# First layer's convolution inputs and output gate as float32 products, decays and half the key rope issued earlier

## The chip, the cores and the metric

The kernel runs on one core of one Trainium2 chip. The metric is the device time of one execution in microseconds, median of three; lower is better. Names of engines: PE is TensorE (matmul), PEld its weight load, DVE VectorE, ACT ScalarE, POOL GpSimd, SP the engine that issues nearly all DMAs.

## The reference, cut to what matters

A decoder of two layers for 256 tokens of width 1024. Each layer is a token mixer and then a SwiGLU FFN of hidden width 2816, both between RMSNorms and modulated by a conditioning vector `c` through a large weight `w_mod`.

```python
# mixer, group A: sparse attention, 8 heads x 64
idx_logits = einsum('thd,sd->ths', q_idx, k_idx)      # indexer, 8 heads
idx_score  = einsum('ths,th->ts', relu(idx_logits), w_idx)
sel        = top_k(causal(idx_score), 64)             # keys kept per query
out_a      = softmax(q.k[sel] / 8) @ v[sel]           # q, k with rotary embedding
# mixer, group B: mLSTM, 4 heads x 128, chunks of 64
qm, km     = silu(causal_dwconv(h @ W_qm)), silu(causal_dwconv(h @ W_km))
out_b      = mlstm_chunkwise(qm, km, vm, igate, log_sigmoid(fgate)) * sigmoid(h @ W_om)
y          = concat(head_norm(out_a), head_norm(out_b)) @ w_out
# FFN
y          = (silu(h @ w_gate) * (h @ w_up)) @ w_down
```

`h` is the normed and modulated input, 256 x 1024, kept as 8 blocks of 128 features. `W_qm`, `W_km` and `W_om` are column blocks of one input projection; each is 1024 x 512.

## The kernel before

**Two forms of a product.** Most products are made of three float32r matmuls: both operands are split into a high part (cast to float32r) and a low part (the difference), and `mm3` (L107 to L111) adds high x high, high x low and low x high in PSUM. `split_half` (L92 to L102) makes the parts of half a weight tile, 128x1024: the high part by ACT (L90), the low part (L101) by DVE, or by POOL where the split is marked `aside`. In the first layer the early products (values, index keys, latent queries, keys) are plain float32 products on `hf`, the unsplit `h`, with unsplit weights. Four of the products of this layer still use the split form: the two convolution inputs (`qk`, through `feat`; two weight tiles `wqk` each, PSUM m0pqk) and the output gate (`gate`, through `tok_half` and `tok`; two tiles `wom`, PSUM m0pom). For these `h` itself is split at L472 to L475 in four ACT casts and four DVE subtractions.

**Buffers.** Weight tiles of 1 MB come through the pool `ring` (7 buffers), one DMA each, issued by SP in the order of the program; a load waits until the instructions that read the tile formerly in its slot are done. Parts go to the pool `split` (5 high, 5 low). So a tile of weights that are split is free once its splits are done, a raw tile once PE has used it. PSUM has two pools of four banks.

**Order.** The mixer is cut into steps with one letter each: `e` the second half of the attention keys with the index products inside, `i` scores and top-k, `r` the key rope, `w` the mLSTM decays, `l` attention logits, `t` softmax and transposes of the weights, `u` values, `a` attended output and its norm, `q` and `k` convolution inputs, `z` silu, `m` memory, `n` recall, `s` scales, `o` gate, `g` gated, `c` and `h` transposes into the concatenation, `y` output projection; `b` and `d` are portions of a stream from `w_mod` of a later modulation (tiles `wm`, sums `macc` on DVE). The string `ORDER[0]` sets their order in the program. A step without `~` is pinned behind the last matmul of the step before; one with `~` is placed by the scheduler of the framework at build time, which fixes the order of instructions on each engine. On the chip each engine runs its list in that order, and an instruction whose operands aren't ready holds all behind it on its engine.

Names: m0 is the first layer's mixer, f0 its FFN. m0pka are attention keys in PSUM, m0pi index products, m0sc scores, m0mk the mask of the top-k, m0rka0p and m0rka0b (and 1) the two halves of the key rope on PE and DVE, m0kT the rotated keys, m0pl logits, m0lm masked logits, m0pT transposed weights, m0cv convolutions, m0W memory weights, m0num recall, m0y the projection.

## Time and profile before

| | us |
|---|---|
| median of 3 executions (754.1 to 756.5) | 754.64 |
| profiled execution | 756.11 |
| its span | 754.2 |
| PE busy | 706.8 (94%) |
| DVE busy | 569.6 (76%) |
| ACT busy | 361.3 (48%) |
| POOL busy | 120.1 (16%) |

The span runs from the first to the last instruction of the execution. An engine is busy while an instruction of it executes; a wait stands with the instruction that waited and is put down to what ended it. The granted clock of TensorE is given as a share of 2.4 GHz, so 0.5 is the level of 1.2 GHz. The prefixes h and l at the end of a weight's name are its high and low part; the digits name the tile and the half.

### The profile page before, as it was taken

How to read it: one execution, taken by the hardware profiler on the slowest of the kernel's cores; microseconds unless marked ns; L12 is line 12 of the kernel's file. 1: busy time of each engine (PE TensorE's matmuls, PEld its weight loads, DVE VectorE, ACT ScalarE, POOL GpSimd, SP SyncE). 2: the span in 40 equal slices, each digit the busy share in tenths (PEclk: the TensorE clock that was granted, in tenths of full speed). 3: DMA queues.
4: the chain of work that ended last, by engine and by line, in shares of the span. 5: the costliest groups of instructions: out<-in, count | busy, mean ns of one | idle time of the engine just before them, and what ended most of it. 6: DMA issues, size and time to landing. Idle time of an engine off the chain costs nothing.

```text
span 754.2 us, 11854 instructions
## 1 busy us (share of the span) xinstructions
PE 706.8 (94%) x4677; PEld 624.9 (83%) x4677; DVE 569.6 (76%) x870; ACT 361.3 (48%) x629; POOL 120.1 (16%) x99
## 2 busy tenths in 40 slices
PE   3989979978999999999989989999999999999996
PEld 2338748968789999999978978899879999999995
DVE  4587898997888856888797999978777576555553
ACT  6132434847474444443534543586765444444442
POOL 1000632321100013120011162633120000000020
PEclk9999978999999999999998999999999999999998
DMA  9999961265868975968785863143464587575101
GB/s 305 355 336 385 326 223 59 65 218 166 306 223 308 335 259 185 335 245 317 276 282 184 269 228 118 58 167 113 141 221 169 168 291 268 186 261 168 56 1 56
DMA packets 106156, 162.79 MB, mean 216 GB/s; under 512 B 7587, under 2 KB 83951, under 8 KB 106101
## 3 DMA queue, kind: packets, MB, share of 16 engines
q1 hardware_dynamic: 106100, 162.04, 62.8%
q8 instruction: 37, 0.61, 0.3%
q14 instruction: 19, 0.15, 0.1%
HBM read 160.98 MB, written 1.05 MB: 215 GB/s over the span
## 4 chain that ended last, share of the span: by engine, by line
PE 63%; DVE 15%; issue 9%; DMA 6%; POOL 3%; ACT 3%; SPq 0%; DVEq 0%; POOLq 0%; ACTq 0%
PE f1pu L111 8%; PE f1pg L111 8%; PE f1y L111 7%; PE f0pg L111 5%; PE f0y L111 4%; PE f0pu L111 4%; DMA wm<-in_w_mod_dram 4%; PE m1pqk L111 3%; PE m1y L111 3%; DVE macc L191 3%; PE pvm L111 2%; PE pva L111 2%; PE m0pqk L111 2%; PE m1pom L111 1%; DMA f0wd<-in_w_down_dram 1%
## 5 line engine op out<-in xcount | busy, mean ns | idle before, releaser
L191 DVE SCALAR_TENSOR_TENSOR macc<-wm,ccol,macc 128x1024 f32<-128x1024 f32 x70 | 93.9, 1341 | 9.4 <-DMA wm<-in_w_mod_dram 8.8
L258 POOL TENSOR_TENSOR macc<-macc,br 1x512 f32<-1x512 f32 x6 | 8.6, 1435 | 170.9 <-DMA br<-in_b_mod_dram 148.5
L111 PE MATMUL pvm<-m0wvm,n0hf 128*128 128x512 f32 x32 | 17.1, 684 | 7.2 <-ACT n0hf L966 5.5
L208 DVE SCALAR_TENSOR_TENSOR macc<-wq,ccol,macc 128x512 f32<-128x512 f32 x28 | 21.1, 752 | 1.2 <-DMA wq<-in_w_mod_dram 0.2
L111 PEld LDWEIGHTS pvm<-m0wvm,n0hf 128*128 128x128 f32 x32 | 6.7, 219 | 15.4 <-ACT n0hf L966 7.4
L882 ACT CAST f0th<-f0t 128x512 fp32r<-128x512 f32 x10 | 6.2, 620 | 22.7 <-DVE f0t L872 22.7
L966 ACT ACTIVATE n0hf<-n0xT,mod,A 128x256 f32<-128x256 f32 x7 | 3.9, 594 | 27.2 <-DVE A L220 27.2
L111 PE MATMUL m0pka<-n0hf,m0wka 128*128 128x256 f32 x64 | 15.9, 389 | 0.0
L111 PE MATMUL pva<-m0wva,n0hf 128*128 128x512 f32 x32 | 14.4, 592 | 0.0
L111 PEld LDWEIGHTS m0pka<-n0hf,m0wka 128*128 128x128 f32 x64 | 11.5, 190 | 3.3 <-issue 1.6
L189 DVE TENSOR_SCALAR macc<-wm,ccol 128x1024 f32<-128x1024 f32 x10 | 8.9, 888 | 6.5 <-DMA wm<-in_w_mod_dram 5.2
L872 DVE TENSOR_TENSOR f1t<-f1pu,f1s 128x512 f32<-128x512 f32 x11 | 7.6, 690 | 6.7 <-PE f1pu L111 5.2
L262 POOL TENSOR_TENSOR ml<-macc,mh 128x512 fp32r<-128x512 f32 x6 | 9.6, 1592 | 19.3 <-ACT mh L260 19.3
L111 PEld LDWEIGHTS pva<-m0wva,n0hf 128*128 128x128 f32 x32 | 6.1, 190 | 7.7 <-issue 7.2
L101 POOL TENSOR_TENSOR f0wd910l<-f0wd,f0wd910h 128x1024 fp32r<-128x1024 f32 x1 | 2.6, 2647 | 59.2 <-ACT f0wd910h L90 59.2
L354 POOL TENSOR_TENSOR m0qidx<-m0rqidx0x,cosT 128x512 f32<-128x512 f32 x1 | 1.5, 1547 | 65.1 <-ACT m0rqidx0x L90 65.1
L770 DVE SCALAR_TENSOR_TENSOR m1cv<-m1pqk,vc,m1cv 128x255 f32<-128x255 f32 (+2 forms) x24 | 11.1, 476 | 0.7 <-ACT m1cv L764 0.5
L101 POOL TENSOR_TENSOR f0wd201l<-f0wd,f0wd201h 128x1024 fp32r<-128x1024 f32 x1 | 2.4, 2409 | 57.8 <-ACT f0wd201h L90 57.8
L770 DVE SCALAR_TENSOR_TENSOR m0cv<-m0pqk,vc,m0cv 128x255 f32<-128x255 f32 (+2 forms) x24 | 10.9, 470 | 0.0
L115 PE MATMUL pm<-ident,macc 128*128 128x128 f32 x72 | 10.4, 283 | 0.4 <-ACT row L90 0.4
L115 PE MATMUL n0pt<-ident,n0xr 128*128 128x128 f32 x16 | 3.9, 428 | 7.2 <-ACT n0xr L317 7.2
L218 DVE TENSOR_REDUCE mod<-pm 128x4 f32<-128x512 f32 x4 | 2.8, 692 | 10.2 <-PE pm L115 10.2
(1917 smaller groups left out, 2978.1 us busy)
## 6 DMA issues: line engine op xcount, KB each, us to landing
wm<-in_w_mod_dram SPq DMA_DIRECT2D x40, 1024.0 KB
f0wd<-in_w_down_dram SPq DMA_DIRECT2D x11, 1024.0 KB
f1wd<-in_w_down_dram SPq DMA_DIRECT2D x11, 1024.0 KB
f0wg<-in_w_gate_up_dram SPq DMA_DIRECT2D x10, 1024.0 KB
f0wu<-in_w_gate_up_dram SPq DMA_DIRECT2D x10, 1024.0 KB
f1wg<-in_w_gate_up_dram SPq DMA_DIRECT2D x10, 1024.0 KB
f1wu<-in_w_gate_up_dram SPq DMA_DIRECT2D x10, 1024.0 KB
wq<-in_w_mod_dram SPq DMA_DIRECT2D x32, 256.0 KB
```

The lines of the kernel that those rows point to most:

```text
L101: final["lo"] = (nc.gpsimd if aside != (name in OTHER) else nc.vector).tensor_tensor(lv, raw, hv.bitcast(F32), op=ALU.subtract)
L111: final["pe"] = nc.tensor.matmul(*args, **kw)
L115: final["pe"] = nc.tensor.transpose(*args)
L189: nc.vector.tensor_scalar_mul(acc, w[:, kk, :], ccol[:, k:k + 1])
L191: nc.vector.scalar_tensor_tensor(acc, w[:, kk, :], ccol[:, k:k + 1], acc, op0=ALU.mult, op1=ALU.add)
L208: last = nc.vector.scalar_tensor_tensor(acc, w[:, kk, :], ccol[:, k:k + 1], acc, op0=ALU.mult, op1=ALU.add)
L258: nc.gpsimd.tensor_tensor(acc[0:1, :], acc[0:1, :], br[0:1, :], op=ALU.add)
L262: nc.gpsimd.tensor_tensor(lo, acc, hi.bitcast(F32), op=ALU.subtract)
L770: nc.vector.scalar_tensor_tensor(o[:, d:], s[:, :S - d], V["conv_w"][:, tap * 8 + j:tap * 8 + j + 1], o[:, d:], op0=ALU.mult, op1=ALU.add)
L872: nc.vector.tensor_mul(t, pu, s)
L882: nc.scalar.copy(th[:, 0], r3(t, 2))
L966: nc.scalar.activation(hf[:, j, :], s, AF.Identity, scale=A, bias=b)
```

## The change

`hf` takes the place of the split `h` (its tag "hh"; the tile "hl" stays, without use in this layer's mixer), the pool `ring` gets an eighth buffer, and `h` is not split. The convolution inputs and the output gate of the first layer become float32 products of `hf` and raw tiles: no parts of `wqk` and `wom` are made. `ORDER[0]` starts with the decays (`w0`) and the first half of the key rope (`r0`) ahead of the index products (`e10`, `e11`); its second half (`r1`) loses its pin, and `k00` and `q00` stand ahead of `l0`.

```diff
--- before.py
+++ after.py
@@ -57,7 +57,7 @@
 def tile_hybrid_decoder(ctx: ExitStack, tc: tile.TileContext, a, out):
     nc = tc.nc
     const = ctx.enter_context(tc.tile_pool(name="const", bufs=1))
-    ring = ctx.enter_context(tc.tile_pool(name="ring", bufs=7))
+    ring = ctx.enter_context(tc.tile_pool(name="ring", bufs=8))
     split = ctx.enter_context(tc.tile_pool(name="split", bufs=5))
     keep = ctx.enter_context(tc.tile_pool(name="keep", bufs=1))
     work = ctx.enter_context(tc.tile_pool(name="work", bufs=2))
@@ -383,13 +383,16 @@
     def tok_split(raw, nm):
         return [split_half(raw[:, 4 * g:4 * g + 4, :], f"{nm}{g}", g == 1) for g in range(2)]
 
-    def tok(ps, ws, h, tiles, inside=()):
+    def tok(ps, ws, h, tiles, inside=(), hf=None):
         step, inside, wait = 0, dict(inside), None
         for i in tiles:
             for k in range(KD):
-                w = ws[k // 4]
+                w = ws[k // 4] if hf is None else None
                 hold = tc.issue_after(wait) if wait else ExitStack()
                 with hold:
+                    if hf is not None:
+                        matmul(ps[:, i * 256:(i + 1) * 256], hf[:, k, i * P:(i + 1) * P], ws[:, k, :], start=k == 0, stop=k == KD - 1)
+                        continue
                     mm = mm3(ps[:, i * 256:(i + 1) * 256],
                              (h[0][:, k, i * P:(i + 1) * P], h[1][:, k, i * P:(i + 1) * P]),
                              (w[0][:, k % 4, :], w[1][:, k % 4, :]), k == 0, k == KD - 1)
@@ -435,7 +438,7 @@
                     first and q == 0, last and q == len(ws) - 1)
 
     HEAD = ((2, 2, 1, 1), (3, 2, 1, 0, 0))
-    ORDER = ("e10~ e11~ i0~ r0~ b1~ i1~ w0~ r1 l0~ t00~ k00~ q00~ l1 t01 q01 d u00~ l2 b1 u01 t10~ t11 u10 k01~ d a0~ q10 z0~ t20~ q11 u11 t21~ u20~ k10~ u21 k11 a1 b1 c0~ d b2~ z1~ m0 n0 o00~ c1~ o01~ m1 n1~ o10~ s0~ b1 s1 o11 g1 g0~ d h1~ h0 y0~ y2~",
+    ORDER = ("w0~ r0~ e10~ e11~ i0~ b1~ r1~ i1~ k00~ q00~ l0~ t00~ l1 t01 q01 d u00~ l2 b1 u01 t10~ t11 u10 k01~ d a0~ q10 z0~ t20~ q11 u11 t21~ u20~ k10~ u21 k11 a1 b1 c0~ d b2~ z1~ m0 n0 o00~ c1~ o01~ m1 n1~ o10~ s0~ b1 s1 o11 g1 g0~ d h1~ h0 y0~ y2~",
              "v0 i0 r0 r1~ i1 w0~ v1~ l0 k00~ l1 b1 q00 t01~ t00~ q01~ u00 t10 b0 l2~ u01~ t11~ q10 b0 k01 u10~ a0~ t20 q11~ u11 c0 u20~ t21 k10 b1~ u21 b0~ k11~ z0 m0 z1 b0 o00~ a1~ o01~ n0~ m1~ c1 n1~ o10 s0~ o11~ g0~ y0 s1 g1~ h0 h1 y2~")
 
     def mixer(l, h, between, early, hook, hf=None):
@@ -469,10 +472,6 @@
         else:
             with tc.issue_after(final["A"].ins):
                 angles()
-                for q in range(4):
-                    two = slice(2 * q, 2 * q + 2)
-                    nc.scalar.copy(h[0][:, two, :], hf[:, two, :])
-                    nc.vector.tensor_tensor(h[1][:, two, :], hf[:, two, :], h[0][:, two, :].bitcast(F32), op=ALU.subtract)
         for k in range(KD):
             if l:
                 mm3(ps[:80, :S], (hi[:, k, :], lo[:, k, :]), (h[0][:, k, :], h[1][:, k, :]), k == 0, k == KD - 1)
@@ -539,8 +538,9 @@
 
         def tok_half(key, c0, name, tile_, inside=()):
             if tile_ == 0:
-                half[key] = bankB(f"{nm}p{name}"), tok_split(load_cols(win, c0, f"{nm}w{name}"), f"{nm}w{name}")
-            tok(*half[key], h, (tile_,), inside)
+                raw = load_cols(win, c0, f"{nm}w{name}")
+                half[key] = bankB(f"{nm}p{name}"), tok_split(raw, f"{nm}w{name}") if l else raw
+            tok(*half[key], h, (tile_,), inside, hf)
             return r3(half[key][0], 2)
 
         def v_att(g, tile_, inside=()):
@@ -755,7 +755,7 @@
             if m == 0:
                 half[key] = bankB(f"{nm}pqk{which}{g}"), load_cols(win, (C_QM, C_KM)[which] + g * 256, name)
             ps, raw = half[key]
-            feat(ps, raw, h, name, True, None, (m,))
+            feat(ps, raw, h, name, True, None, (m,), (), hf)
             if m == 0:
                 return
             for m in range(2):
@@ -947,13 +947,12 @@
     little(2)
     xT = first_norm("n0")
     keep.tile([P, 16], F32, tag="edge0", name="edge0")
-    h = hh, hl = new_h("n0")
+    hf = keep.tile([P, KD, S], F32, tag="hh", name="n0hf")
+    keep.tile([P, KD, S], F32R, tag="hl", name="n0hl")
     keep.tile([P, 48], F32, tag="edge1", name="edge1")
     A0 = small.tile([P, KD], F32, tag="A1", name="A0")
     macc0 = [work.tile([P, D], F32, tag="macc", name=f"macc0{t}", bufs=2) for t in range(2)]
     early = {n: [bankB(f"p{n}{i}") for i in range(NT)] for n in ("vm", "va")}
-    hf = keep.tile([P, KD, S], F32, tag="hf", name="n0hf")
-
     for q in range(4):
         B = mod_quarter(q)
         wv = {n: r3(split.tile([P, 1024], F32, tag=t, name=f"m0w{n}{q}"), 2) for n, t in (("vm", "hi"), ("va", "lo"))}
@@ -1014,7 +1013,7 @@
 
         if l + 1 < L:
             turns_of.append(load_vectors(1))
-        y = mixer(l, h, during[l][0], early, to_ffn, None if l else hf)
+        y = mixer(l, h if l else None, during[l][0], early, to_ffn, None if l else hf)
         h = next_h(y, rowsof[l, G_M], rowsof[l, SC_F], mod_of(l, SH_F), f"nf{l}")
         y = ffn(l, h, during[l][1], nxt["w"], to_mixer)
         if l + 1 < L:
```

The scheduler places the instructions anew. On PE, from the last index product (m0pi) of the first mixer on, the list before is this (m0pu and m0pM belong to the mLSTM decays):

```order
L111 MATMUL m0pi_649<-m0kidx,m0qidx 128x256 x2
L111 MATMUL m0pka_589<-n0hf,m0wka_590 128x256 x4
L111 MATMUL m0rka0p<-m0rka0x,perm 128x512
L115 MATMUL m0pu<-ident,m0ga 128x4 x4
L111 MATMUL m0pM_743<-Mp,sel 128x256 x2
L111 MATMUL m0pM_753<-Mp,sel 128x256 x2
L111 MATMUL m0pqk_803<-n0hh,m0wqk100l 128x256
L111 MATMUL m0pqk_803<-n0hh,m0wqk100h 128x256
L111 MATMUL m0pqk_803<-n0hl,m0wqk100h 128x256
L111 MATMUL m0pqk_803<-n0hh,m0wqk100l 128x256
L111 MATMUL m0pqk_803<-n0hh,m0wqk100h 128x256
L111 MATMUL m0rka1p<-m0rka1x,perm 128x512
```

and in the changed kernel, from the same product up to the first transposes of the attention weights:

```order
L111 MATMUL m0pi_675<-m0kidx,m0qidx 128x256 x2
L111 MATMUL m0pka_615<-n0hf,m0wka_616 128x256 x4
L111 MATMUL m0pqk_762<-n0hf,m0wqk_763 128x256 x2
L111 MATMUL m0rka1p<-m0rka1x,perm 128x512
L111 MATMUL m0pqk_762<-n0hf,m0wqk_763 128x256 x3
L111 MATMUL m0pqk_773<-n0hf,m0wqk_774 128x256 x8
L111 MATMUL m0pl_787<-m0kT,m0q 128x128 x4
L111 MATMUL m0pl_793<-m0kT,m0q 128x128 x4
L111 MATMUL m0pqk_762<-n0hf,m0wqk_763 128x256 x8
L115 MATMUL m0pT_809<-ident,m0lm_786 128x128 x4
```

m0rka0p, m0pu and m0pM have gone from this place, to one ahead of the first index product; between m0rka1p and the first transposes m0pT now stand 19 steps of m0pqk on the raw tiles and eight products m0pl. On DVE, at the scores of the same mixer, the list before has m0rka0b and the copy of m0uc between the rounds of the first top-k:

```order
L665 MATCH_REPLACE m0sc_594<-m0m_666,m0sc_594 128x128
L654 SCALAR_TENSOR_TENSOR m0sc_621<-m0rl_652,m0wi,m0sc_621 128x256
L664 MAX m0m_669<-m0sc_594 128x8
L356 TENSOR_TENSOR m0rka0b<-m0rka0p,sinT 128x512
L665 MATCH_REPLACE m0sc_594<-m0m_669,m0sc_594 128x128
L357 TENSOR_TENSOR m0kT<-m0kT,m0rka0b 128x512
L664 MAX m0m_672<-m0sc_594 128x8
L611 COPY m0uc<-m0pu 128x8
L665 MATCH_REPLACE m0sc_594<-m0m_672,m0sc_594 128x128
L356 TENSOR_TENSOR m0rka1b<-m0rka1p,sinT 128x512
```

and the changed kernel has them ahead of the first score:

```order
L356 TENSOR_TENSOR m0rq0b<-m0rq0p,sinT 128x512
L356 TENSOR_TENSOR m0rq1b<-m0rq1p,sinT 128x512
L611 COPY m0uc<-m0pu 128x8
L357 TENSOR_TENSOR m0q<-m0q,m0rq1b 128x512
L356 TENSOR_TENSOR m0rka0b<-m0rka0p,sinT 128x512
L357 TENSOR_TENSOR m0kT<-m0kT,m0rka0b 128x512
L652 TENSOR_SCALAR m0sc_620<-m0rl_626,m0wi 128x128
L654 SCALAR_TENSOR_TENSOR m0sc_620<-m0rl_626,m0wi,m0sc_620 128x128
L191 SCALAR_TENSOR_TENSOR macc_498<-wm_890,ccol,macc_498 128x1024
L654 SCALAR_TENSOR_TENSOR m0sc_620<-m0rl_626,m0wi,m0sc_620 128x128
```

m0rka0b, the addition to m0kT and the copy now stand ahead of all scores, and no low part of m0wqk stands there. On DVE at the end of the mixer, from the low parts of the concatenation on (m0wo are weights of the projection, f0we early weights of the FFN), the list before is:

```order
L685 SCALAR_TENSOR_TENSOR m0cat4hl<-m0cm1p,vc_102,m0cat4hh 128x128 x4
L685 SCALAR_TENSOR_TENSOR m0cat4hl<-m0cm0p,vc_102,m0cat4hh 128x128 x4
L101 TENSOR_TENSOR m0wo200l<-m0wo_1606,m0wo200h 128x1024
L101 TENSOR_TENSOR f0we01l<-f0we_1638,f0we01h 128x1024
L101 TENSOR_TENSOR m0wo201l<-m0wo_1606,m0wo201h 128x1024
L101 TENSOR_TENSOR m0wo210l<-m0wo_1608,m0wo210h 128x1024
L101 TENSOR_TENSOR m0wo211l<-m0wo_1608,m0wo211h 128x1024
L101 TENSOR_TENSOR f0we10l<-f0we_1648,f0we10h 128x1024
L101 TENSOR_TENSOR f0we11l<-f0we_1648,f0we11h 128x1024
L302 TENSOR_TENSOR nf0yg_1708<-m0y_1534,row_1021 128x512
L189 TENSOR_SCALAR macc_2186<-wm_2187,ccol 128x1024
```

and the changed kernel's:

```order
L685 SCALAR_TENSOR_TENSOR m0cat4hl<-m0cm1p,vc_102,m0cat4hh 128x128 x4
L685 SCALAR_TENSOR_TENSOR m0cat4hl<-m0cm0p,vc_102,m0cat4hh 128x128 x4
L101 TENSOR_TENSOR f0we01l<-f0we_1389,f0we01h 128x1024
L101 TENSOR_TENSOR m0wo201l<-m0wo_1357,m0wo201h 128x1024
L101 TENSOR_TENSOR m0wo210l<-m0wo_1359,m0wo210h 128x1024
L189 TENSOR_SCALAR macc_1937<-wm_1938,ccol 128x1024
L101 TENSOR_TENSOR m0wo211l<-m0wo_1359,m0wo211h 128x1024
L101 TENSOR_TENSOR f0we10l<-f0we_1399,f0we10h 128x1024
L101 TENSOR_TENSOR f0we11l<-f0we_1399,f0we11h 128x1024
L191 SCALAR_TENSOR_TENSOR macc_1937<-wm_1938,ccol,macc_1937 128x1024
L302 TENSOR_TENSOR nf0yg_1459<-m0y_1285,row_932 128x512
```

The first macc of the tile `wm` now stands ahead of m0wo211l; before it stood behind the first product nf0yg of the next norm.

## Rows read from the trace of the kernel before

**Rows 1.** Windows: us, busy time and instructions by engine, clock, DMA.
```profile
core 0: us, PE busy (x) PEld busy (x) DVE busy (x) ACT busy (x) POOL busy (x), PEclk, DMA share, GB/s
87.00:205.90 118.90, 105.96 (x656) 90.21 (x654) 103.17 (x207) 64.28 (x145) 31.25 (x24) 0.93 0.52 177
103.50:109.00 5.50, 0.29 (x3) 0.12 (x1) 5.50 (x16) 0.00 (x0) 2.06 (x3) 0.64 1.05 356
109.00:119.00 10.00, 10.00 (x38) 7.62 (x39) 8.93 (x31) 2.92 (x10) 2.91 (x6) 0.51 0.14 42
130.00:155.00 25.00, 24.61 (x212) 23.69 (x211) 23.19 (x43) 19.25 (x40) 6.79 (x3) 1.00 0.33 113
155.00:167.00 12.00, 6.81 (x51) 6.26 (x50) 10.88 (x23) 4.71 (x12) 4.01 (x2) 0.98 0.58 206
167.00:184.50 17.50, 15.43 (x113) 14.67 (x111) 13.09 (x29) 12.35 (x32) 2.01 (x2) 0.92 0.56 182
217.10:388.00 170.90, 170.90 (x1245) 161.82 (x1245) 134.43 (x132) 78.32 (x92) 17.05 (x10) 1.00 0.80 278
```

**Rows 2.** Waits of PE from 80 to 225 us, by releaser.
```profile
engine line waited for: us in total, times, longest us
PE m0rka1p L111 <- DVE m0rka0b L356: 5.2, 1, 5.2
PE m0num L111 <- DVE m0W L785: 3.3, 1, 3.3
...
PE m0cm1p L115 <- DVE m0mo L828: 2.1, 1, 2.1
PE m0pqk L111 <- DVE m0cv L770: 1.9, 1, 1.9
```

**Rows 3.** Chain of waits, 62 to 325 us: start, duration, work.
```profile
69.48 5.61 PE m0pka L111 x26
...
108.91 2.04 PE m0rka1p L111 x2
...
123.60 0.11 PE m0pT L115
...
251.96 5.66 PE f0pg L111 x48
```

**Rows 4.** Time line of DVE in the first mixer: start, duration, instruction.
```profile
85.01 0.68 DVE L357 TENSOR_TENSOR m0qidx<-m0qidx,m0rqidx1b 128x512 f32<-128x512 f32 x1
...
87.41 1.21 DVE L101 TENSOR_TENSOR m0wqk100l<-m0wqk,m0wqk100h 128x1024 fp32r<-128x1024 f32 x1
...
91.01 2.83 DVE L357 TENSOR_TENSOR m0q<-m0q,m0rq1b 128x512 f32<-128x512 f32 x1 [1.79 <-POOL m0q L354]
...
97.06 0.27 DVE L652 TENSOR_SCALAR m0sc<-m0rl,m0wi 128x128 f32<-128x128 f32 x1
...
115.59 0.22 DVE L667 TENSOR_SCALAR m0mk<-m0sc 128x128 f32<-128x128 f32 x1
...
128.77 0.29 DVE L667 TENSOR_SCALAR m0mk<-m0sc 128x256 f32<-128x256 f32 x1
...
145.32 2.34 DVE L746 TENSOR_TENSOR m0rd<-m0rd,m0ra0r 128x8 f32<-128x8 f32 x1 [1.55 <-POOL m0ra0r L280]
```

**Rows 5.** Time line of POOL, one low part of a weight.
```profile
90.93 2.36 POOL L101 TENSOR_TENSOR m0wqk001l<-m0wqk,m0wqk001h 128x1024 fp32r<-128x1024 f32 x1
```

**Rows 6.** Chain of waits, then time line of PE, at the projection.
```profile
192.93 7.35 DMA wm<-in_w_mod_dram
...
198.20 0.40 PE L111 MATMUL m0y<-m0wo211l,m0cat4hh 128*128 128x512 f32 x1
```

**Rows 7.** Time lines of DVE, then PE, at the FFN's end.
```profile
367.56 1.23 DVE L101 TENSOR_TENSOR m1wvm00l<-m1wvm,m1wvm00h 128x1024 fp32r<-128x1024 f32 x1 [4.59 <-ACT m1wvm00h L90]
...
392.47 2.60 DVE L191 SCALAR_TENSOR_TENSOR macc<-wm,ccol,macc 128x1024 f32<-128x1024 f32 x2
394.98 1.22 DVE L101 TENSOR_TENSOR f0wd911l<-f0wd,f0wd911h 128x1024 fp32r<-128x1024 f32 x1
...
396.25 0.79 PE L111 MATMUL f0y<-f0wd911l,f0th 128*128 128x512 f32 x1 [2.91 <-DVE f0wd911l L101]
...
397.27 0.63 PE L111 MATMUL f0y<-f0wd910h,f0th 128*128 128x512 f32 x1
...
402.69 0.39 PE L111 MATMUL f0y<-f0wd910h,f0th 128*128 128x512 f32 x1
```

## The prediction, written before the changed kernel ran

> **What bounds the kernel now.** I read four views in this order. First the windows of the stretch that the change touches, the mixer of the first layer [rows 1]: from 87 to 205.9 us TensorE is busy for 105.96 of 118.9 us; most of the rest lies in 103.5 to 109 (0.29 of 5.5 us) and in 155 to 167 (6.81 of 12 us); behind the first hole the granted clock is 0.51, which is the 1.2 GHz level, through all of 109 to 119. VectorE is full in the first hole (5.50 of 5.5) and 91% busy in the second. Then the waits of TensorE [rows 2]: 5.2 us for the key's rotary product m0rka0b, 3.3 us for the memory weights m0W, 1.9 us for the convolutions m0cv, all from VectorE. So the mixer has two limits that alternate: TensorE by its amount of work, VectorE by what stands ahead of the instruction that TensorE needs. Third the chain of waits for the durations [rows 3], fourth the time lines of VectorE and GpSimd around the two holes [rows 4, 5]. Behind the mixer, the FFN from 217 to 388 us keeps TensorE busy for every microsecond [rows 1], so a gain of the mixer arrives at the end unshortened; the one hole of the FFN is at its end [rows 7].
>
> **1. TensorE gets more work: +7.5 us.** 96 products of one contraction step (64 of the convolution inputs, 32 of the output gate) change from three float32r matmuls to one float32 product. The chain has both forms with 256 columns: 13 float32 steps of m0pka (26 records) in 5.61 us, 0.432 us each; 16 steps of three of f0pg in 5.66 us, 0.354 us each [rows 3]. The difference, 0.078, times 96 is 7.5 us. The Trainium skill, "FP8 and Floating Point Precision" (TensorE Precision Notes), says that a true float32 product takes four passes; three passes in 0.354 us would make four 0.472 and the sum 11.3, an estimate by that page, 3.8 us worse than mine. The row measures the very operand kinds, partitions and columns of the new products, and it gives 0.432.
>
> **2. VectorE, ScalarE and GpSimd get less.** Twelve low parts of weights go, six on VectorE at 1.21 us (7.3 us) and six on GpSimd, as do 12 casts on ScalarE and the split of h. The split of h I cost at nothing: it lies before 87 us, where TensorE is busy without a hole for the early products. A GpSimd split also held VectorE: the add to m0q took 2.83 us beside m0wqk001l where an add of the same shape takes 0.68, and m0wqk000l stood beside the next one; m0rd, a 128x8 product, took 2.34 us beside a split of wom [rows 4, 5]. At about 2.2 us each, four such places are 8.7 us. Together VectorE loses 16 us of 103 busy between 87 and 205.9. This is no gain by itself; it counts only where TensorE waits.
>
> **3. The first hole goes: -5.**  In the new order the first half of the key rope, with decays, is issued ahead of the index products. m0rka0b then stands on VectorE ahead of the scores instead of behind the third round of the top-k, where it ran at 108.10 us. What is issued between 87 and 103.5 us on TensorE is otherwise the same work, so m0rka1p comes when the last m0pka and two steps of m0pqk are done, at about 104.4 instead of 108.91 [rows 3]. That is 4.5 us, and the half clock of the 10 us behind it (TensorE is busy there for 10.00 us at 0.51, so 4.9 us of work at full clock [rows 1]) goes as well, if no new hole takes its place.
> One does. TensorE now has ready: 11 steps of m0pqk (4.75 us), the eight m0pl (about 2) and eight more steps (3.46), which brings it to about 115. Then stand the transposes of the weights, which need the exponentials, which need mask 0 and the maximum. VectorE starts the scores at about 92 instead of 97.06, because the two blocked instructions before it are gone; it cannot finish them before the last m0pi, which is now at 101.8 (three instructions were put ahead). I get mask 0 at about 109 instead of 115.59, the maximum at 116.3, the first transposes between 117 and 118.7. So TensorE waits about 3 us there, and probably runs slowly behind it: the only 3.3 us hole of this mixer (before m0num) left 0.92 in the 17.5 us behind it, the 5.2 us hole 0.51 over 10 us [rows 1, 2]. Bounds for the new hole: 0 to 5.2 us, its half clock 0 to 4.9 us; I take 3 and 2. The first transpose was at 123.60 [rows 3] and TensorE has done the same 24 steps before it, so at this point the lead is 5 us (118.7), or 3 with the slow clock behind it.
>
> **4. The second hole shrinks.** Behind the transposes 72 of the 96 longer steps are still to come. In 130 to 155 TensorE is 98% busy [rows 1], so 40 of them lie on the path: 40 x 0.078 = 3.1 us, and the lead at the last convolution product falls from 5 to about 2. But then TensorE was waiting for VectorE: 5.19 of 12 us idle in 155 to 167. VectorE's second mask was at 128.77 [rows 4] and is now at about 118.5. In 130 to 167, up to m0W, it was busy for 34.1 us [rows 1], two blocked m0rd with 4.4 of them, so 29.7 of work; in the new order it has 2.4 us of splits of wo and 2.6 of macc more in front of m0W (they stood behind it) and 1.2 less of wom: 33.5, so it is done by 152, or by 156 with the waits it had, and the last convolution product arrives at 151 to 152 with 3 us of work behind it. m0num starts at about 156 instead of 166.5. From there TensorE had 39.2 us to the end of the output projection, 2.1 of them idle and some 1.4 lost to the clock; with 2.5 us more for the gate that is 39 to 42. The projection ends at 197 to 199 instead of 205.7.
>
> **5. A wait that the order brings in.** The slot for the weight tile wm that is loaded near the end of the mixer is freed by the low part f0we01l, and its first use on VectorE now stands two instructions behind that, ahead of m0wo211l; before it stood well behind it. That load took 7.35 us from issue to landing [rows 6]. Queued behind the waiting macc is m0wo211l, for which TensorE waits: its first use was at 198.20 [rows 6]. Moved by one low part ahead, f0we01l frees the slot at 191.54 of the old time; landing after 4 to 7.35 us (the lower end: the loads ahead of it are released earlier by TensorE now, and 1 MB at the 278 GB/s of [rows 1] takes 3.8), then 0.76 for the macc and 1.23 for the low part, gives 197.5 to 200.9. TensorE waits 0 to 2.7 us; I take 1.
> Parts 3 to 5 together: the walk gives -6.7 to -8.7, less 1. I take -6, since each of its stations assumes no wait that I have not seen; bounds 0 (all holes only move) and -10 (both holes and the half clock go).
>
> **6. The eighth ring buffer: -4.** At the end of the first FFN the last low part f0wd911l starts at 394.98, behind two macc (2.60 us), and TensorE waits 2.9 us; the matmuls behind it start 0.43 us apart until 402, then 0.227 apart, about 12 x 0.2 = 2.4 us more [rows 7]. VectorE has no hole between 367.56 and that point but 0.69 us, and the row at 367.56 shows why it is late: 4.59 us for a cast of a tile that had just landed. The ring has one buffer more, so this load can be issued one slot earlier; where slots and not the transfer rate set the time (0.80 of the DMA share in this stretch, 278 GB/s against 356 in 103.5 to 109 [rows 1]) it lands earlier. In the new order one of the two macc also stands in front of f0th, in the 0.69 us hole. Bounds: 0 (the transfers are the limit) to -5.3 (wait and slow clock go); I take -4, since two microseconds more of the 4.59 already bring the hole to the size (1.9, before m0pqk) behind which the granted clock stayed up. The second layer's mixer and FFN I cost at nothing: the code is the same there.
>
> **Sum.** The profiled execution took 756.11 us with a span of 754.2, so 1.9 us lie around the span. 756.1 - 6 - 4 = 746.1 by that execution; it stands 1.5 us above the median of 754.64, so I forecast **744.6**.
>
> **Rivals.**
> A. The forecast, both gains in part: 741 to 749. Chance 0.50. The page's four passes would put 3.8 us on the sum and stay in this case.
> B. The eighth buffer gives nothing, as the transfers pace the FFN: only the mixer's -6, 754.64 - 6 = 748.6, say 748 to 752. For it speaks the DMA share of 0.80 with transfers of about 7 us; against it that slots are held back by VectorE, which is what waits. Chance 0.23.
> C. The hole at the transposes takes the place of the first one at full price (5.2 and 4.9 us), so the mixer gains 0 to 2, with half the buffer's gain: 750 to 754. For it speaks that TensorE runs out of ready work at 115 at the latest; against it that mask 0 is earlier by six. Chance 0.14.
> D. Slower: TensorE is the bound. The hole moves from m0rka1p to the transposes with its slow clock, as in C, and the 7.5 us of longer products stand on the path all through, since the remaining idle time (3.3, 1.9 and 2.1 us) is in places where the longer products do not fit; about half of it absorbs some. With the wait of part 5 (2.7) and no gain of the buffer: 7.5 + 2.7 - 3.6 = +6.6, 761; from 757 if a part is absorbed. It decides at one point: whether m0num comes later than 164 in spite of the lighter VectorE. Chance 0.08.
> E. VectorE was the bound all through and its 16 us count to the full: -10 and -5, 739.6. Against it TensorE's 98% in 130 to 155. Chance 0.05.
> What a measurement of this kernel can tell from no change is 0.3%, 2.3 us. Faster by more: A, E, nearly all of B (0.20) and a third of C: 0.80. Within: the rest of B and C, 0.12. Slower: 0.08. The range that leaves out D, half of E and a little more is 739.5 to 753.
>
> **What would show it.** Right: m0rka1p at about 104 with no wait; the first score at about 92, mask 0 at about 109; the granted clock near 1 in 105 to 115; m0num at about 156; the end of the projection at 197 to 199; f0wd911l no longer waited for, or for under 2 us. Wrong: a wait of the transposes of over 4 us with the lower level behind it (C); m0num after 164 (D); m0wo211l waited for by over 3 us; the wait for f0wd911l still at 2.9 (B); float32 steps of m0pqk at more than 0.45 us.

## The result: faster by 2.4%

The changed kernel takes 737.4 us (median, 735.65 to 738.5); the kernel before took 755.57 beside it. The ratio is 0.9758, 95% interval 0.9729 to 0.9787. The forecast was 744.6, the range 739.5 to 753. So the direction was right, and the gain is 18 us where 10 were forecast; the time lies 2.1 us below the range. The profiled execution has a span of 735.2 us, 19.0 less than before. The ratios in this document leave out executions over 1.5% above the fastest of their kernel (among them four of the twelve of f2 below and one of the twelve of f3), while the medians in us are of all executions.

Where the 19.0 us come from is read by following the same instructions in both traces: the last m0y ends 8.8 us earlier (197.03 for 205.83), all FFN matmuls behind the norm run 11.5 earlier, the last f0y ends 18.1 earlier (388.36 for 406.48), the last instruction 19.0. So up to the end of the mixer 8.8 us are gained, in the norm behind it 2.7, at the end of the first FFN 6.6, in the second layer 0.9. The 8.8 hold a loss of 1.8 from the start of the execution, told below; from the last matmul of pva (it ends at 57.74 for 55.93) to the end of m0y the gain is 10.6.

The windows of the kernel after, by the columns of [rows 1]; the first is its mixer from the place of the old 87 us to the end of m0y, the second the norm behind it:

```profile
core 0: us, PE busy (x) PEld busy (x) DVE busy (x) ACT busy (x) POOL busy (x), PEclk, DMA share, GB/s
88.80:197.03 108.23, 105.96 (x559) 86.44 (x558) 91.02 (x204) 54.52 (x134) 14.80 (x17) 1.00 0.63 211
197.03:205.10 8.07, 6.89 (x56) 6.43 (x57) 7.54 (x19) 7.41 (x19) 1.10 (x2) 1.00 0.62 216
106.70:119.00 12.30, 11.58 (x59) 9.18 (x58) 11.85 (x40) 1.02 (x5) 1.57 (x2) 1.00 0.30 92
...
372.00:388.40 16.40, 16.36 (x73) 13.17 (x71) 11.47 (x14) 7.05 (x15) 3.51 (x3) 1.00 0.96 330
```

The mixer is 108.23 us long; the same stretch before, 87 to 205.85, was 118.85. TensorE was busy for 105.96 us of either. It was idle for 12.89 us and is for 2.27: the shortening is idle time, all of it. That busy time has not grown although the products are longer goes, by an estimate from these rows, to the clock: it was 0.93 over the stretch of [rows 1] and is 1.00 now, and 7% of 106 us is 7.4, about the 7.5 us of the longer products. The norm takes 8.07 us for 11.25, and the end of the FFN (372 to 388.4) has no hole and the full clock. The waits of TensorE from 60 to 480 us (columns as in [rows 2]), against those there and in [rows 7]:

```profile
PE nf0pt L115 <- DVE nf0xr L332: 1.2, 2, 0.7
...
PE m0pT L115 <- ACT m0lm L711: 0.7, 1, 0.7
...
PE m0cm1p L115 <- DVE m0mo L828: 0.4, 1, 0.4
```

The 5.2, 3.3 and 1.9 us are gone, 2.1 has become 0.4, and the 2.9 us at the end of the FFN are gone too. TensorE's stations, for [rows 3] (start and duration of a group; the idle time before it in brackets):

```profile
106.70 1.13 PE L111 MATMUL m0rka1p<-m0rka1x,perm 128*128 128x512 f32 x2
...
118.53 1.48 PE L115 MATMUL m0pT<-ident,m0lm 128*128 128x128 f32 x4 [0.66 <-ACT m0lm L711]
...
154.08 0.83 PE L111 MATMUL m0num<-m0vm,m0W 128*128 128x129 f32 x6
```

and VectorE's, for [rows 4], at the index products and at the end of the mixer:

```profile
91.01 1.26 DVE L357 TENSOR_TENSOR m0q<-m0q,m0rq1b 128x512 f32<-128x512 f32 x1
...
94.24 0.42 DVE L652 TENSOR_SCALAR m0sc<-m0rl,m0wi 128x128 f32<-128x128 f32 x1
...
110.77 0.21 DVE L667 TENSOR_SCALAR m0mk<-m0sc 128x128 f32<-128x128 f32 x1
...
178.43 1.21 DVE L101 TENSOR_TENSOR f0we01l<-f0we,f0we01h 128x1024 fp32r<-128x1024 f32 x1
182.88 1.23 DVE L101 TENSOR_TENSOR m0wo201l<-m0wo,m0wo201h 128x1024 fp32r<-128x1024 f32 x1 [3.24 <-ACT m0wo201h L90]
...
185.38 0.75 DVE L189 TENSOR_SCALAR macc<-wm,ccol 128x1024 f32<-128x1024 f32 x1
```

The add to m0q is down from 2.83 to 1.26 us, the first score at 94.24, mask 0 at 110.77. All of these times hold 1.8 us from the start of the execution: eight early matmuls of pvm took 5.40 us where before they took 3.70. The first line is from the kernel before, the others are from the changed kernel, the last with the columns of [rows 1]:

```profile
39.52 3.70 PE L111 MATMUL pvm<-m0wvm,n0hf 128*128 128x512 f32 x8 [1.81 <-ACT n0hf L966]
...
39.63 5.40 PE L111 MATMUL pvm<-m0wvm,n0hf 128*128 128x512 f32 x8 [1.87 <-ACT n0hf L965]
...
39.60:43.00 3.40, 3.37 (x5) 1.35 (x6) 3.26 (x5) 0.47 (x1) 0.00 (x0) 0.55 1.01 340
```

So the lag is the lower level of the clock (0.55 over 3.4 us) behind a hole of 1.87 us; before, the hole was 1.81 us and the clock stayed at 1.00. Whether it comes from the change is open: of the nine traces in which no split `h` is made (the changed kernel and the runs e1, e2, e5, e6, f1, f2, f3 and g1 below), all have the hole of 1.87 us, but seven have the 5.40 us and two, f2 and g1, have 3.70; the five traces that split `h` have 1.81 and 3.70.

### The profile page after: what moved, and what is told of

The parts are those of the page before. It is cut to its first block, busy times and chain, and to the rows that moved or that the text cites. A ratio compares the mean times of both kernels' runs of the same rounds, so it can differ in the third digit from the quotient of the medians.

```text
span 735.2 us, 11619 instructions
## 1 busy us (share of the span) xinstructions
PE 702.1 (95%) x4581; PEld 618.8 (84%) x4581; DVE 550.9 (75%) x860; ACT 348.3 (47%) x613; POOL 106.3 (14%) x93
## 4 chain that ended last, share of the span: by engine, by line
PE 80%; DVE 11%; ACT 3%; issue 3%; POOL 1%; DMA 1%; SPq 0%; DVEq 0%; POOLq 0%; ACTq 0%
PE f1pu L111 8%; PE f0pu L111 8%; PE f0pg L111 8%; PE f1pg L111 8%; PE f1y L111 7%; PE f0y L111 7%; PE m1pqk L111 3%; PE m1y L111 3%; PE pvm L111 3%; PE m0y L111 2%; PE pva L111 2%; PE m0pka L111 2%; PE m1pva L111 2%; PE m1pom L111 1%; PE m1pka L111 1%
## 5 line engine op out<-in xcount | busy, mean ns | idle before, releaser
L191 DVE SCALAR_TENSOR_TENSOR macc<-wm,ccol,macc 128x1024 f32<-128x1024 f32 x70 | 96.1, 1373 | 9.5 <-DMA wm<-in_w_mod_dram 8.8
L111 PE MATMUL m0pqk<-n0hf,m0wqk 128*128 128x256 f32 x128 | 29.6, 382 | 0.0
L111 PEld LDWEIGHTS m0pqk<-n0hf,m0wqk 128*128 128x128 f32 x128 | 23.8, 190 | 3.6 <-issue 0.5
L111 PEld LDWEIGHTS pvm<-m0wvm,n0hf 128*128 128x128 f32 x32 | 7.1, 234 | 16.4 <-ACT n0hf L965 7.7
L111 PE MATMUL m0pom<-m0wom,n0hf 128*128 128x256 f32 x64 | 14.5, 379 | 0.0
L111 PEld LDWEIGHTS m0pka<-n0hf,m0wka 128*128 128x128 f32 x64 | 11.5, 190 | 3.3 <-issue 1.6
L111 PEld LDWEIGHTS m0pom<-m0wom,n0hf 128*128 128x128 f32 x64 | 11.9, 190 | 1.4
L711 ACT ACTIVATE m0lm<-m0lm,m0mx 128x128 f32<-128x128 f32 (+1 forms) x16 | 7.1, 445 | 12.2 <-DVE m0mx L708 12.2
```

The costliest lines, as they stand in the source:

```text
L111: final["pe"] = nc.tensor.matmul(*args, **kw)
L191: nc.vector.scalar_tensor_tensor(acc, w[:, kk, :], ccol[:, k:k + 1], acc, op0=ALU.mult, op1=ALU.add)
L711: final["exp"] = nc.scalar.activation(lm[:, g, :], lm[:, g, :], AF.Exp, bias=mx[:, g:g + 1], accum_out=den[:, hd:hd + 1])
```

## Experiments

Each kernel was timed in turns with the kernel before on the same chip; the ratio to it is what is compared (medians of before lie between 753.9 and 755.6 us).

| run | products | order string | buffers | else | us | ratio (95%) |
|---|---|---|---|---|---|---|
| changed kernel | float32 | new | 8 | | 737.4 | 0.9758 (0.9729 to 0.9787) |
| e1_ring7 | float32 | new | 7 | | 745.0 | 0.9869 (0.9832 to 0.9905) |
| e2_oldorder | float32 | old | 8 | | 737.6 | 0.9767 (0.9736 to 0.9798) |
| e3_before_neworder | split | new | 7 | | 757.4 | 1.0028 (1.0004 to 1.0052) |
| e5_f32only | float32 | old | 7 | | 745.4 | 0.9884 (0.9848 to 0.9920) |
| f1_keep_all | float32 | old | 7 | all splits made, and six that the kernel before lacks | 765.8 | 1.0149 (1.0116 to 1.0181) |
| f2_keep_pool | float32 | old | 7 | GpSimd's splits made, and three more | 756.8 | 0.9995 (0.9962 to 1.0028) |
| f3_keep_dve | float32 | old | 7 | VectorE's splits made, and three more | 750.4 | 0.9935 (0.9902 to 0.9969) |
| h1_conv_only | float32 in conv | old | 7 | | 750.6 | 0.9937 (0.9912 to 0.9962) |
| h2_gate_only | float32 in gate | old | 7 | | 750.6 | 0.9934 (0.9908 to 0.9960) |
| e6_ring6 | float32 | new | 6 | | 743.5 | 0.9847 (0.9806 to 0.9888) |
| g1_ring7_macc_last | float32 | new | 7 | last macc late | 738.3 | 0.9784 (0.9756 to 0.9812) |
| i1_before_macc_last | split | old | 7 | last macc late | 750.4 | 0.9953 (0.9930 to 0.9977) |

### Which part of the change: products, order or buffer

```diff
e1:  -ring bufs=8  +ring bufs=7                       (of the changed kernel)
e2:  -ORDER[0] new +ORDER[0] of before                (of the changed kernel)
e3:  -ORDER[0]     +ORDER[0] of the changed kernel    (of the kernel before)
e5:  e1 and e2 together
```

e1_ring7. 

> The changed kernel with 7 ring buffers instead of 8. Theory (the buffer makes the gain at the end of the first FFN, the rest of the change makes that of the mixer): the wait for f0wd911l returns with 2 to 3.5 us and a slow clock behind it, the end of the projection m0y stays near 197 us; 741 to 745 us, 4 to 7 above the changed kernel's 737.4. Rival (the macc moved ahead of f0th, or the earlier start of the stream, makes the gain at the FFN's end): no wait there, 737 to 739 us.

e2_oldorder. 

> The changed kernel with the order string of before (float32 products and 8 buffers stay). Theory (products and order share the mixer's gain, since the lighter VectorE reaches m0rka0b earlier even where it stands among the top-k rounds): a hole of 1 to 3 us before m0rka1p, m0num near 158 to 160, the FFN's end without a wait; 740 to 744 us. Rival (the order alone makes the mixer's gain, the longer products only cost): the hole of 5 us and the slow clock stay, 748 to 755 us.

e3_before_neworder. 

> The kernel before with the order string of the change alone (split form, 7 buffers). Theory: m0rka0b comes early and the hole of 5 us goes, but VectorE keeps its splits and its blocked instructions, so m0num waits as before; mixer 2 to 5 us shorter, the wait at the FFN's end stays: 750 to 754 us. Rival (the order alone makes the mixer's gain): the projection ends near 197 us, 743 to 748 us.

e5_f32only. 

> The float32 products alone: order string of before, 7 ring buffers. Theory: as the run with the old order and 8 buffers, but with the wait at the FFN's end: 745 to 751 us. Rival (TensorE's work bounds the mixer, 7.5 us more of it): 755 to 762 us.

The products alone give 1.2% (e5), the eighth buffer another 1.1% (e1 against the changed kernel, e5 against e2), the order nothing: with it or without it the float32 kernels are equal within their intervals, at either number of buffers, and alone (e3) it costs 0.3%. For e2 my theory still left 1 to 3 us of the hole to the order; its wait is this:

```profile
PE m0rka1p L111 <- DVE m0rka0b L356: 0.4, 1, 0.4
```

With the old order m0rka0b still stands among the top-k rounds, but VectorE gets there in time. For e3 both expectations were wrong. The first hole is gone there and three others have come, in places that had none or less before: two wait for VectorE directly, and m0pT waits for ScalarE's m0lm, which needs VectorE's mask. The third line is the FFN's end, as it was:

```profile
PE m0pqk L111 <- DVE m0cv L770: 4.9, 1, 4.9
PE m0pl L111 <- DVE m0kT L357: 3.5, 1, 3.5
PE f0y L111 <- DVE f0wd911l L101: 2.9, 1, 2.9
PE m0pT L115 <- ACT m0lm L711: 2.6, 1, 2.6
```

So the place of m0rka0b decides where TensorE waits, but gains nothing: VectorE was late, and with the new order other instructions of TensorE waited for it.

### What in the products: VectorE's own work or GpSimd's hold on it

```diff
 # e5, in feat (and alike for wom in tok_half); the parts are read by nothing
             if hf is None:
                 w = ... split_half(...)
+            elif True:          # f1; f2: m == 1 (GpSimd's), f3: m == 0 (VectorE's)
+                split_half(raw[:, :, m * P:(m + 1) * P], f"{nm}{m}", aside and m == 1)
```

f1_keep_all. 

> The float32 products alone (old order, 7 buffers; 745.4 us), and the twelve splits of wqk and wom made all the same, for nothing: six low parts on VectorE, six on GpSimd, twelve casts on ScalarE. TensorE's matmuls are those of the changed kernel. Theory (the mixer's gain is the work taken from VectorE, and TensorE's longer products only cost): the hole before m0rka1p and the wait for m0W return, 753 to 760 us. Rival (the gain comes from TensorE's side: fewer and simpler matmuls, or raw tiles freed in another order): 744 to 748 us.

f2_keep_pool. 

> As the run that keeps all splits, but only the six low parts on GpSimd with their six casts. Theory (GpSimd's splits hold VectorE for about 2.2 us each in four places): about half of the loss returns, m0q and m0rd take over 2 us again; 748 to 751 us. Rival (only VectorE's own work counts): 744 to 747 us.

f3_keep_dve. 

> As the run that keeps all splits, but only the six low parts on VectorE (1.21 us each) with their six casts. Theory: the other half, 748 to 752 us. Rival (GpSimd's blocking makes the loss): 744 to 747 us.

These three runs make more splits than their expectations count. `feat` also makes the latent queries and the attention keys, whose weights m0wcq and m0wka the kernel before never splits. So f1 makes eighteen splits and not twelve, f2 and f3 nine each and not six, and the scheduler put them at other times than in the kernel before (m0wqk011l on GpSimd at 101.73 in f2, at 119.89 before). What they show is the direction: TensorE's products are those of e5 in all three, and with split work added the gain shrinks (f3, where 0.5% are lost against e5) or is gone (f2, where 1.1% are lost, though its splits use no time of VectorE's own). What pays is the work taken away, not the form of the product. What the six splits of each engine cost they don't show: before any low part of m0wqk is made, VectorE's m0qidx already comes 3.7 us later than in e5 in f2, and 2.8 later in f3 (both counted from the last pva), where m0rka0b in the end is 6.8 and 4.2 us later. The casts on ScalarE and the buffers of `split` that these splits take were not tested apart. In f2 the wait before m0rka1p is back, larger than before; the other rows are a GpSimd split and, on VectorE, a score instruction that runs into it and the like one that doesn't:

```profile
PE m0rka1p L111 <- DVE m0rka0b L356: 6.1, 1, 6.1
...
101.73 2.36 POOL L101 TENSOR_TENSOR m0wqk011l<-m0wqk,m0wqk011h 128x1024 fp32r<-128x1024 f32 x1
...
102.00 2.37 DVE L659 SCALAR_TENSOR_TENSOR m0sc<-m0rl,m0wi,m0sc 128x256 f32<-128x256 f32 x1
...
107.09 0.47 DVE L659 SCALAR_TENSOR_TENSOR m0sc<-m0rl,m0wi,m0sc 128x256 f32<-128x256 f32 x1
```

2.37 us for 0.47: the instruction of VectorE lasts until the split of GpSimd is over. In f3 the same wait of TensorE is 2.5 us. f1 lost more than f2 and f3 together, and more than was expected, but not by the splits of the change. The pair m0wi took 0.36 us in the kernel before; in f1 it runs into GpSimd's split of m0wka and lasts 3.63, VectorE's own split of m0wka follows, m0qidx comes late by both, TensorE waits 2.75 us ahead of m0pi, and the lower clock follows; columns of the window as above:

```profile
87.82 3.63 DVE L594 TENSOR_SCALAR m0wi<-m0wif,m0rqr 128x8 f32<-128x8 f32 x2
...
87.85 2.35 POOL L101 TENSOR_TENSOR m0wka11l<-m0wka,m0wka11h 128x1024 fp32r<-128x1024 f32 x1
...
87.00:120.00 33.00, 30.25 (x80) 19.49 (x78) 30.96 (x40) 11.70 (x16) 17.68 (x11) 0.64 0.37 120
...
95.03 1.22 PE L111 MATMUL m0pi<-m0kidx,m0qidx 64*128 64x128 f32 x4 [2.75 <-DVE m0qidx L357]
96.18 2.07 PE L111 MATMUL m0pka<-n0hf,m0wka 128*128 128x256 f32 x4
```

Two float32 steps of m0pka take 2.07 us there where they take 1.06 on the chain after, and this lasts from 95 to 119 us (granted clock 0.50), so by an estimate up to 12 us of this run's loss are the clock.

### Which of the products

```diff
h1 (of before):  qk():  -feat(ps, raw, h, name, True, None, (m,))
                        +feat(ps, raw, h, name, True, None, (m,), (), hf)
h2 (of before):  tok and tok_half as in the changed kernel; qk and the split of h stay
```

h1_conv_only. 

> The kernel before with the convolution inputs alone as float32 products (h is split still, for the gate; old order, 7 buffers). Theory (the low parts of wqk stand ahead of m0rka0b, and make the first hole): nearly the whole gain of the products, hole under 1 us, 745 to 749 us. Rival (the parts of wom in the second hole count as much): 749 to 752 us.

h2_gate_only. 

> The kernel before with the output gate alone as float32 products (h and wqk split still; old order, 7 buffers). Theory: the first hole of 5 us stays, the wait for m0W falls by 2 to 3 us, TensorE has 2.5 us more: 752 to 756 us, no difference that can be told. Rival: 749 to 752 us.

Each gives about 0.65%, and together they are what e5 gives: the rivals were right. Both runs still split `h`, and e5 doesn't; nothing is left over that this split could be worth. The conv products remove the first hole (m0rka0b at 101.69 on VectorE, 2.1 us of that from an earlier start of this execution; the wait for it is 0.4 us) and leave waits further on:

```profile
PE m0pqk L111 <- ACT row L90: 2.4, 2, 2.2
...
101.69 0.67 DVE L356 TENSOR_TENSOR m0rka0b<-m0rka0p,sinT 128x512 f32<-128x512 f32 x1
```

The gate leaves the first hole as it was, and gains behind it: m0rd, which took 2.34 us beside a wom split, takes 0.17, and the waits for m0W and m0cv are gone. From the last pva its m0y ends 3.0 us earlier, and the norm behind it is 2.6 shorter, of which h1 has 0.3 (more on the norm below):

```profile
PE m0rka1p L111 <- DVE m0rka0b L356: 5.2, 1, 5.2
...
145.92 0.17 DVE L750 TENSOR_TENSOR m0rd<-m0rd,m0ra0r 128x8 f32<-128x8 f32 x1 [1.54 <-POOL m0ra0r L280]
```

### The end of the first FFN: the buffer or VectorE's list

```diff
e6:  -ring bufs=8  +ring bufs=6                       (of the changed kernel)
 # g1 (of e1) and i1 (of the kernel before), in ffn
-            between()
+            if c < NF - 2 or l:
+                between()
...
         down(NF - 2, NF - 1)
+        if not l:
+            between()
```

e6_ring6. 

> The changed kernel with 6 ring buffers (8: 737.4, 7: 745.0 us). Theory (slots, not the transfer rate, set when the FFN's tiles come): each buffer less costs about as much, the waits of TensorE in the FFN grow to 6 us or more; 752 to 765 us. Rival (7 buffers are just one short of what the end of the FFN needs and the transfer rate bounds the rest): 745 to 749 us.

g1_ring7_macc_last. 

> The changed kernel with 7 buffers (745.0 us, waits 2.9 us for f0wd911l at the end of the first FFN), and the last portion of the w_mod stream of that FFN written behind the last down product: its two macc (2.6 us) then stand behind f0wd911l on VectorE. Theory A (the wait is VectorE's queue, 27 us without a hole from the late tile m1wvm to f0wd911l; 2.6 us out of it do nearly what the eighth buffer does): wait for f0wd911l 0 to 1 us, no slow clock, 738 to 741 us. Theory B (the late tile itself, thus the slot, is what counts): the wait stays over 2 us, 743 to 746 us.

i1_before_macc_last. 

> The kernel before, with the last portion of the w_mod stream of the first FFN written behind the last down product and nothing else of the change. Theory (the wait at the FFN's end is VectorE's queue ahead of f0wd911l; the eighth buffer is one way to shorten it): no wait of TensorE there, 747 to 751 us. Rival (without the buffer or the faster mixer the tiles come too late): the wait stays over 2 us, 753 to 757 us.

With 7 buffers the wait of 2.9 us is back; first line TensorE's wait, then VectorE from the late tile on:

```profile
PE f0y L111 <- DVE f0wd911l L101: 2.9, 1, 2.9
...
358.35 1.23 DVE L101 TENSOR_TENSOR m1wvm00l<-m1wvm,m1wvm00h 128x1024 fp32r<-128x1024 f32 x1 [4.66 <-ACT m1wvm00h L90]
...
385.59 1.22 DVE L101 TENSOR_TENSOR f0wd911l<-f0wd,f0wd911h 128x1024 fp32r<-128x1024 f32 x1
```

In the changed kernel the cast of that tile is through at 347.81 and f0wd911l starts before TensorE needs it:

```profile
347.81 1.23 DVE L101 TENSOR_TENSOR m1wvm00l<-m1wvm,m1wvm00h 128x1024 fp32r<-128x1024 f32 x1 [2.39 <-ACT m1wvm00h L90]
...
377.30 1.23 DVE L101 TENSOR_TENSOR f0wd911l<-f0wd,f0wd911h 128x1024 fp32r<-128x1024 f32 x1 [0.16 <-ACT f0wd911h L90]
```

But e6, with one buffer less than e1, has no such wait, and is no slower than e1; both its expectations were wrong. From the last f0pu to the last f0y it takes 16.4 us as the changed kernel does, where e1 takes 23.4; its mixer ends 2.5 us later than that of e1 (1.0 of it from the start of the execution), its norm is 2.2 longer and its second layer 2.4. Its scheduler put a pair of macc behind f0wd911l instead of ahead of it:

```profile
365.35 1.23 DVE L101 TENSOR_TENSOR m1wvm00l<-m1wvm,m1wvm00h 128x1024 fp32r<-128x1024 f32 x1 [0.40 <-ACT m1wvm00h L90]
...
386.03 1.21 DVE L101 TENSOR_TENSOR f0wd911l<-f0wd,f0wd911h 128x1024 fp32r<-128x1024 f32 x1
...
389.32 2.61 DVE L191 SCALAR_TENSOR_TENSOR macc<-wm,ccol,macc 128x1024 f32<-128x1024 f32 x2 [0.95 <-DMA wm<-in_w_mod_dram]
```

g1 does that by hand with 7 buffers, and is as fast as the changed kernel within the intervals; TensorE waits for f0wd911l no more:

```profile
349.64 1.23 DVE L101 TENSOR_TENSOR m1wvm00l<-m1wvm,m1wvm00h 128x1024 fp32r<-128x1024 f32 x1 [0.21 <-ACT m1wvm00h L90]
...
375.78 1.22 DVE L101 TENSOR_TENSOR f0wd911l<-f0wd,f0wd911h 128x1024 fp32r<-128x1024 f32 x1 [0.16 <-ACT f0wd911h L90]
376.93 1.28 DVE L191 SCALAR_TENSOR_TENSOR macc<-wm,ccol,macc 128x1024 f32<-128x1024 f32 x1
```

i1 does it in the kernel before, with nothing else changed. The first wait, 5.2 us, and the second, 3.5, are there still as in [rows 2]; the one at the FFN's end was 2.9 us:

```profile
PE f0y L111 <- DVE f0wd911l L101: 0.2, 1, 0.2
...
363.88 1.23 DVE L101 TENSOR_TENSOR m1wvm00l<-m1wvm,m1wvm00h 128x1024 fp32r<-128x1024 f32 x1 [2.46 <-ACT m1wvm00h L90]
...
390.52 1.21 DVE L101 TENSOR_TENSOR f0wd911l<-f0wd,f0wd911h 128x1024 fp32r<-128x1024 f32 x1
```

Its f0y ends 7.1 us earlier, of which 6.1 fall between the last f0pu and the last f0y, and 6.6 in the changed kernel; only 0.5%, some 3.5 us, shows in the ratio. The second layer is 1.6 us longer in its trace; where the rest goes is open.

So TensorE stands at the end of VectorE's list: in e1 that is 27 us with one hole of 0.69 from the late tile to f0wd911l. The runs do not show that the moved macc shorten this list. In the kernel before, e1, the changed kernel, g1 and i1 alike, eight macc stand between m1wvm00l and f0wd911l, and it takes 26 to 29 us: for the two that g1 and i1 move, two come in that stood ahead of the late tile. What differs is its start. Counted back from the end of the last f0pu, m1wvm00l starts 15.9 us earlier in the kernel before and 14.3 in e1, which wait, and 24.2 in the changed kernel, 20.8 in g1 and 18.6 in i1, which don't. With the portion that g1 and i1 move, one load of a tile wm has gone from ahead of m1wvm in SP's list, and the first load of m1wvm is issued at 342.58 in g1 (350.31 in e1, whose execution was 2.1 us later from the start) and at 354.55 in i1 (359.59 before). So the time came out as theory A of g1 said, but not by its mechanism, and g1 and i1 don't decide between list and slot. For the list speaks e6 alone: m1wvm00l starts 13.5 us ahead there, as late as in e1, but the list has six macc and 20.7 us, and TensorE doesn't wait. No run moved the macc without the load. The eighth buffer is one way to this gain, not the only one.

## Why the prediction was wrong

**Right.** The price of the longer products: eight steps of the gate on the chain after,

```profile
154.92 3.45 PE m0pom L111 x16
```

are 0.431 us each, 0.432 was forecast. Of the walk's stations, with the lag of 1.8 us in them: the first score at 94.24 (92 forecast), mask 0 at 110.77 (109), m0rka1p at 106.70, which is the 104.4 with the lag and half a microsecond more, the first transposes at 118.5 (117 to 118.7), the end of the projection at 197.03 (197 to 199). m0num at 154.08 (156) is no like point: in the kernel before some 12 steps of the gate stood ahead of m0num, and in the changed kernel all stand behind it, so that from m0num on it took 42.95 us where 39 to 42 were walked. e2, which has 11 steps ahead of it, reaches m0num at 158.93 and the end of the projection at 197.10. That the walk still ends near the mark is partly luck. That the GpSimd splits hold VectorE was right, and the wait that returns in f2 shows it; which engine's splits were the larger half, the runs don't show.

**The step that failed most: "I take -6".** The walk of parts 3 and 4 gave -6.7 to -8.7, and I cut it for waits that I had not seen. Its last sum was already too small: m0num at 156 and 39 to 42 us behind it make 195 to 198, not 197 to 199, so its own terms gave -7.7 to -10.7. The end of m0y moved by -8.8, by -10.6 without the lag, which is beyond the bound of -10. What I had put in as costs was not there: the new hole at the transposes was 0.66 us instead of 3, with no lower clock behind it instead of 2 us; and the wait of part 5 was nothing. On that wait the slot was freed by f0we01l as said, but the next instruction, m0wo201l, waited 3.24 us for its cast, so VectorE came to the macc 5.7 us after the slot was free, and the tile was there.

**A term that was missing: the norm.** The forecast left it as it was, without a reason. It went from 11.25 to 8.07 us, and 2.7 us of that reach the FFN. The two chains of waits, before and after:

```profile
207.75 2.18 ACT nf0hh L339 x8
209.93 0.58 ACT nf0y1j L286 x2
...
210.54 0.22 DVE nf0y1m L290
...
198.29 0.60 DVE nf0yg L302
198.89 0.13 DVE nf0y1m L290
```

Before, ScalarE makes eight parts nf0hh of the norm's first half ahead of nf0y1j, the squares of its second half, and VectorE's nf0y1m waits for them; in the changed kernel nf0y1j stands ahead of nf0hh. In VectorE's list one macc of 1.28 us, at 207.58, is gone from the same place, but the chain does not go through it. From the first to the last transpose nf0pt it is 7.4 us in the changed kernel and in e1, e2, e5, f1, f2, f3, g1 and h2, and 9.7 to 10.0 in the kernel before, e3, e6, h1 and i1: two sizes, that go neither with the buffers nor with the speed of the mixer, but with these two orders in all fourteen traces. No run moved either alone, so their parts are read from the traces, not shown.

**Part 6, a size.** -4 was taken, -5.3 the bound; it was -6.6. The wait of 2.9 us was sized right. Behind it fourteen matmuls ran at the lower level and lost 2.8 us, where 2.4 were counted. And some 0.8 us were lost ahead of the wait, between 390 and 393 us, at full clock, in holes too short for the list of waits; these were not counted. Two windows of the kernel before:

```profile
388.00:393.00 5.00, 4.90 (x21) 3.27 (x19) 4.31 (x6) 1.79 (x3) 0.00 (x0) 1.00 0.80 279
...
396.30:402.00 5.70, 5.70 (x14) 4.44 (x15) 2.87 (x5) 1.38 (x4) 0.56 (x1) 0.50 1.05 370
```

That the buffer lets the late tile come earlier was right; that it takes a buffer was not (g1).

**Part 3, the cause.** I gave the end of the first hole to the new order. e2 and e3 give the gain to the load taken from VectorE; the order is worth nothing. The number came out because both stood in the walk at once. Of the rivals, E (VectorE was the bound all through) was nearest to what happened and had 0.05.

**"The second layer at nothing"** was -0.9, the rest of the sum: 8.8 + 2.7 + 6.6 + 0.9 = 19.0 against 10.

## What to carry to other kernels

When an engine's waits name several different instructions of one other engine, the load of that engine is the bound, and moving one of its instructions only moves the wait; take work off it, or from whatever holds it up, and count the clock that the holes cost as part of the price. Walk the new order through its stations, and then believe the sum: a cut for unseen waits needs a row as much as a gain does. Before a wait is laid to a buffer, look at what stands ahead of the awaited instruction on its engine and in the queue of loads: one portion of background work (a load and two sums) written later did here what a megabyte of buffer did. When work is put back to test a cause, count it in the trace: a helper with other callers can put back more than was taken away.

## What the runs showed of the hardware that was not expected

A hole's length did not tell what it costs in clock: 5.2 us ahead of m0rka1p were followed by 10 us at the 1.2 GHz level [rows 1, 2], 6.1 us at the same place in f2 by some 3 us (0.50 until about 114), 2.8 us ahead of m0pi in f1 by 24 us; and the hole of 1.87 us before the early pvm was followed by the lower level in seven traces and by the full clock in g1 and f2. And splits whose results nobody reads cost 1.1% from GpSimd and 0.5% from VectorE (nine of each, f2 and f3 against e5): the engine that does the work is not the only one that pays.
